# Latent attention's probabilities turned by transposing transfers out of SBUF

## The chip, the cores and the metric

The kernel runs on one core of a Trainium2 chip. A core has five engines, each with its own in-order instruction queue: TensorE (PE; its weight loads are counted apart as PEld), VectorE (DVE), ScalarE (ACT), GpSimd (POOL) and SyncE (SP), which issues transfers. The metric is the device time of one execution in microseconds.

## The reference

A decoder trunk of two layers over 256 rows of width 2048, in f32. Layer 0 has differential attention, layer 1 latent attention; each is followed by cross-attention into 256 memory rows and by a squared-ReLU MLP. The change touches the attention part of layer 1:

```python
def mla_attention(h, wdown, q_norm, kv_norm, wuq, wukv, wo, cos, sin):
    ...
    q = jnp.concatenate([q[..., :MLA_NOPE], apply_rope(q[..., MLA_NOPE:], cos, sin)], axis=-1)
    ...
    def block(qi, q0):
        s = jnp.einsum('bqhd,bkhd->bhqk', qi, k).astype(jnp.float32) * scale
        s = jnp.where(causal_mask(q0, S), s, -jnp.inf)
        p = jax.nn.softmax(s, axis=-1).astype(v.dtype)
        return jnp.einsum('bhqk,bkhd->bqhd', p, v)
```

There are 16 heads of 128 columns plus 64 rotary ones, and query blocks of 128 rows.

## The kernel before

Every product is done in three passes: each f32 operand is split into a high half (a rounded copy, by ScalarE) and a low half (the rest, by VectorE), and high x high, high x low and low x high are added in PSUM. Weights arrive by SP's queue in tiles `raw` of 128 x 2048 (1 MB, seven buffers), and are split in pieces of 1024 columns into `whi` (L221, ScalarE) and `wlo` (L222, VectorE), four buffers of each. TensorE reads one such pair in a run of twelve matmuls of 512 columns; a fifth split waits until the first pair has been read.

Latent attention goes in four groups of four heads (0 to 3). For each group, `project_latent` makes queries, keys and values, `attend4` the attention, and `project_group` adds the group's part of the output projection one group later. Within `attend4` there are four blocks: two pairs of heads p, two query tiles t. Tile t = 0 has 128 keys (256 probabilities a row for a pair), t = 1 has 256 (512 a row). A block (`probs`) does these steps: TensorE's scores into a PSUM bank (`ax`); VectorE's mask, maximum and scale, ScalarE's two exponentials (L619), VectorE's reciprocal and product (L680), which leave the probabilities in a tile `p`; TensorE's flips of `p`, two or four transposes of 128 x 128 (L174, from L684) back into the same bank; ScalarE's high half (L687) and VectorE's low half (L688) into a tile that the products with the values (`weighted`) read.

The queries' rotary parts are turned in the same stretch (`rotary_queries`): GpSimd rotates them, ScalarE copies a rounded half into a tile `ev` (L1721), VectorE adds the rest (L1722), TensorE flips eight blocks of it. The rotary queries of groups 2 and 3 are made while group 1 is in its softmax. During group 3, ScalarE also scales rows of the memory (`memT`, L416) for the next cross-attention.

`p`, `ev`, the `planes` below and some others share one set of seven buffers (EVS).

What sets the order: TensorE's order is the order in which the code emits it. Side tasks (generators) are put between the matmuls of the main stream by a clock of estimated times; a `yield` names the time after which the task may go on (T_SM after a softmax, a slack for each group, T_TURN after a turn). The other engines' queues are ordered at build time by the framework's scheduler, from estimates of its own, and this order is fixed. SP's loads stay in program order. An instruction that waits holds up all that is behind it on its engine.

The kernel has a transposing path through DRAM in other places: ScalarE parts the 16-bit halves of f32 words into two planes (L377), GpSimd writes them to DRAM (L379), SP's transposing transfer brings them back turned (L384).

Of the kernel before, what the change touches and what calls it, by code (L numbers as in the profile page):

```python
# [10 lines left out]
F32 = mybir.dt.float32  # L11
F32R = mybir.dt.float32r
I32 = mybir.dt.int32
U16 = mybir.dt.uint16
# [4 lines left out]
P = 128  # L19
# [3 lines left out]
CH = 512  # L23
# [7 lines left out]
EVS = 7  # L31
# [3 lines left out]
T_EV, T_TURN, T_ROT, T_SM, T_SQ, T_ADD, T_NORM, T_SUM, T_BATCH, T_STORE, T_LAND, T_DMA, T_SHORT = 2.6, 2.6, 12.0, 6.5, 4.4, 2.2, 7.2, 3.0, 17.0, 22.0, 7.0, 8.0, 11.0  # L35

URGENT = 250
NEG = -1.0e30
LAMBDA_INIT = 0.8 - 0.6 * math.exp(-0.3 * 0)
SC_DA = 1.0 / math.sqrt(128)  # L40
# [12 lines left out]
def trunk(ctx, tc, x, xT, xT0, mem, memT, positions, gcols, gfinal, lam_vecs, consts, W, out):  # L53
    nc = tc.nc

    def pool(name, bufs, space=None):
        kw = {"space": space} if space else {}
        return ctx.enter_context(tc.tile_pool(name=name, bufs=bufs, **kw))
# [5 lines left out]
    work = pool("work", 2)  # L64
# [6 lines left out]
    def nm(s):  # L71
        serial[0] += 1
        return f"{s}_{serial[0]}"
# [82 lines left out]
    def side_bank():  # L156
        while not free_banks[0]:
            yield 0.5
        free_banks[0] -= 1
        return bank()  # L160

    def give_back():
        free_banks[0] += 1

    def mmul(o, stationary, moving, start, stop, onto=False):
        n = 1
        for d in moving.shape[1:]:
            n *= d
        clock[0] += max(0.11, n / 2400 + 0.0133)
        return nc.tensor.matmul(o, stationary, moving, start=start, stop=stop, skip_group_check=onto)  # L170

    def flip(o, src):
        clock[0] += 0.109
        nc.tensor.transpose(o, src, ident)  # L174

    def f32(ap):
        return ap.bitcast(F32)
# [6 lines left out]
    def urgent():  # L184

        return tc.high_priority(offset=URGENT)

# [6 lines left out]
    def raw_tile():  # L194
        return wraw.tile([P, 4 * CH], F32, tag="raw", name=nm("raw"))
# [186 lines left out]
    def turned_by_dma(there):  # L382
        landed = work.tile([P, 4, 2 * P], U16, tag="ev", name=nm("landed"), bufs=EVS)
        tc.keep_in_program_order(nc.sync.dma_start_transpose(landed, there))  # L384
        return landed.bitcast(F32).rearrange("p k t -> p k t")

    def split_landed(dst, t, src):
        at = slice(t * P, (t + 1) * P)
        hi = dst[:, 0, :, at]
        tc.keep_in_program_order(nc.scalar.copy(hi, src))  # L390
        nc.vector.tensor_tensor(dst[:, 1, :, at], src, f32(hi), ALU.subtract)  # L391
# [213 lines left out]
    def val(v, half, kb, lo, n):  # L605
        return v[:, half, 2 * kb : 2 * kb + 2, :].rearrange("p a b -> p (a b)")[:, lo : lo + n]
# [33 lines left out]
    def side_by_side(q, k, h):  # L640

        both = k[:, :, h, :P]
        return [(q[:, 0, h], (both,)), (q[:, 1, h], (both,))]

    def scores(view, blocks, t, causal):


        for b, pairs in enumerate(blocks):
            todo = [(q[:, t * P : (t + 1) * P], kk) for q, ks in pairs for kk in ks]
            for i, (q, kk) in enumerate(todo):  # L650
                mmul(view[:, b], q, kk, i == 0, i == len(todo) - 1)
        if causal:
            last = view[..., view.shape[-1] - P :]
            nc.vector.tensor_tensor(last, last, masks(len(blocks)), ALU.add)

    def masks(n):
        return mask.unsqueeze(1).broadcast_to([P, n, P])

    def attend4(score_pairs, inputs, v, dst, causal, scales=(1.0, 1.0), slack=0.0):


        pTs = [raw_tile().bitcast(F32R).rearrange("p (a b c d) -> p a b c d", a=2, b=2, c=2) for _ in range(2)]

        def probs(t, p, nk):


            sb = yield from side_bank()
            heads = (2 * p, 2 * p + 1)
            pr = work.tile([P, CH], F32, tag="ev", name=nm("p"), bufs=EVS)[:, : 2 * nk]
            rows = pr.rearrange("p (h k) -> p h k", k=nk)  # L670
            if nk == P:
                view = sb.rearrange("p (h a k) -> p h a k", h=2, a=2)
                scores(view, [score_pairs(h, True) for h in heads], t, False)
                nc.vector.tensor_tensor(rows, view[:, :, 1], masks(2), ALU.add)
                nc.vector.tensor_tensor(rows, rows, view[:, :, 0], ALU.add)
                pr, rs = softmax(pr, 2, pr, scales[t])
            else:
                scores(sb.rearrange("p (h k) -> p h k", k=nk), [score_pairs(h, False) for h in heads], t, causal)
                pr, rs = softmax(sb, 2, pr, scales[t])
            nc.vector.tensor_tensor(rows, rows, rs[:, :2].unsqueeze(2).broadcast_to([P, 2, nk]), ALU.mult)  # L680
            yield T_SM + slack
            nb = nk // P
            for i in range(2 * nb):
                flip(sb[:, i * P : (i + 1) * P], pr[:, i * P : (i + 1) * P])  # L684
            src = sb[:, : 2 * nk].rearrange("p (h b q) -> p h b q", h=2, b=nb)
            hi = pTs[p][:, 0, :, :nb, t * P : (t + 1) * P]
            nc.scalar.copy(hi, src)  # L687
            nc.vector.tensor_tensor(pTs[p][:, 1, :, :nb, t * P : (t + 1) * P], src, f32(hi), ALU.subtract)  # L688
            give_back()
            yield T_TURN  # L690

        def weighted(po, p, i, kb, passes, first, last):
            vt = v() if callable(v) else v
            q = slice(kb * P if causal else 0, S)
            o = po[:, i * S : (i + 1) * S][:, q]
            for j, (sv, sp) in enumerate(passes):
                mmul(
                    o, val(vt, sv, kb, (2 * p + i) * P, P), pTs[p][:, sp, i, kb, q],
                    first and j == 0, last and j == len(passes) - 1,
                )  # L700

        def result(p, po):
            hi = dst[:, 0, 2 * p : 2 * p + 2, :]
            src = po.rearrange("p (h q) -> p h q", h=2)
            with urgent():
                nc.scalar.copy(hi, src)
                nc.vector.tensor_tensor(dst[:, 1, 2 * p : 2 * p + 2, :], src, f32(hi), ALU.subtract)

        PASSES = ((0, 0), (0, 1), (1, 0))

        def task():
            for i in inputs:
                yield i
            blocks = []
            for p in range(2):
                for t in range(NT):
                    blocks.append(Task(probs(t, p, P if causal and t == 0 else S)))
                    yield 1.3
            for b in blocks:
                yield b  # L720
            if causal:
                for p in range(2):
                    po = yield from side_bank()
                    for i in range(2):
                        for kb in range(2):
                            weighted(po, p, i, kb, PASSES, kb == 0, kb == 1)
                    result(p, po)
                    give_back()
                    yield 1.3
            else:  # L730
                pos_ = []
                for p in range(2):
                    pos_.append((yield from side_bank()))
                while not v():
                    yield 0.5
                for p in range(2):
                    for i in range(2):
                        weighted(pos_[p], p, i, 0, PASSES, i == 0, False)
                for p in range(2):
                    for passes in (PASSES[:2], PASSES[2:]):  # L740
                        for i in range(2):
                            weighted(pos_[p], p, i, 1, passes, False, passes == PASSES[2:] and i == 1)
                    result(p, pos_[p])
                    give_back()
            yield T_TURN

        dst.run(task())
# [859 lines left out]
    krope = Held(raw_tile().bitcast(F32R)[:, : 2 * S].rearrange("p (k t) -> p k t", k=2))  # L1607
# [37 lines left out]
    rq = keep2(rs, SC_MLA, "rq")  # L1645
# [99 lines left out]
    slacks = [4.5, 2.5, 2.5, 2.5]  # L1745

    def attend_latent(held, o):
        qr, q, k, v = held
        attend4(
            lambda h, first: side_by_side(q, k, h) + [(qr[:, h], (krope[:, :, :P],))]  # L1750
            if first
            else whole(q, k, h, S) + [(qr[:, h], (krope[:, 0], krope[:, 1]))],
            qr.tasks + q.tasks + k.tasks + krope.tasks, v, o, True, rq, slacks.pop(0),
        )

    norm, m, mk = attention(project_latent, attend_latent, sooner, G_CROSS + 16)
# [81 lines left out]
def _layout(i):  # L1838
# [16 lines left out]
    c[:, C_ID : C_ID + P] = np.eye(P, dtype=np.float32)  # L1855
    c[:, C_MASK : C_MASK + P] = np.where(q[None, :] <= q[:, None], 0.0, NEG)
    inv = [500000.0 ** (-(np.arange(0, r, 2)) / r) for r in (DA_ROT, MLA_ROPE)]
# [49 lines left out]
```

## Time and profile before

| what | value |
|---|---|
| median of 3 runs | 2172.3 us (2171.3 to 2172.62) |
| profiled execution, first to last instruction | 2169.0 us, granted clock 0.999 |
| TensorE busy | 2155.4 us (99%) |
| weight loads | 1805.5 us (83%) |
| VectorE busy | 1740.2 us (80%) |
| ScalarE busy | 1465.6 us (68%) |
| GpSimd busy | 221.0 us (10%) |
| DMA queue of SP's transfers | 440.14 MB, 56.9% of the span |

The profiled execution is told by its span alone; the runs' times also hold what lies before the first and after the last instruction. Latent attention lies between about 1200 and 1375 us: the scores of groups 0 to 3 begin at 1220, 1251, 1301 and 1348 us. A row of the chain of waits gives a start, a length and what ended last there; a row of instruction groups gives engine, operation, tiles written and read, and durations in ns as least, median and greatest.

### The profile page before, as it was taken

The page shows a single profiled execution, that of the slowest core. Times are in us where ns is not written, and L with a number is a line of the kernel's source. Part 1 is how long each engine was busy: PE and PEld are TensorE (multiplying, and loading weights), DVE is VectorE, ACT ScalarE, POOL GpSimd, SP SyncE. Part 2 cuts the span into 40 slices and gives each one's busy share as a digit, 9 for nine tenths or more (in the row PEclk, how much of TensorE's full clock was granted, in tenths as well). Part 3 has the DMA queues.
Part 4 walks back from the last instruction along what each step waited for, and adds up shares of the span by engine and source line. Part 5 has one row for each costly group of instructions (what it writes and reads, how often), then busy time and mean ns, then how long its engine had stood idle before and what let it go on. Part 6 is the DMA issues. An engine that isn't in the chain of part 4 may idle for free.

```text
span 2169.0 us, 27519 instructions
## 1 busy us (share of the span) xinstructions
PE 2155.4 (99%) x10187; PEld 1805.5 (83%) x10187; DVE 1740.2 (80%) x1962; ACT 1465.6 (68%) x1938; POOL 221.0 (10%) x336
## 2 busy tenths in 40 slices
PE   9999999999999999999999999999999999999998
PEld 7888888888888888888889988888888888888887
DVE  6656878788788889788886878778888888888887
ACT  7556756666767777776665755666777778677665
POOL 1113210001000000000000420000000000000001
PEclk9999999999999999999999999999999999999999
DMA  9477896548989999998986344645998999999895
GB/s 386 151 248 234 260 293 222 194 151 267 297 280 267 308 282 256 319 274 260 306 251 218 103 170 155 221 168 182 283 299 292 258 317 280 266 285 310 254 315 149
DMA packets 151863, 543.89 MB, mean 251 GB/s; under 512 B 79536, under 2 KB 79920, under 8 KB 92848
## 3 DMA queue, kind: packets, MB, share of 16 engines
q1 hardware_dynamic: 134496, 440.14, 56.9%
q0 software_dynamic: 16800, 101.20, 22.5%
q8 instruction: 80, 1.31, 0.2%
q10 hardware_dynamic: 432, 0.79, 0.1%
q14 instruction: 55, 0.45, 0.1%
HBM read 505.38 MB, written 19.40 MB: 242 GB/s over the span
## 4 chain that ended last, share of the span: by engine, by line
PE 95%; DVE 3%; DMA 1%; issue 1%; ACT 0%; DVEq 0%; POOLq 0%; POOL 0%
PE mm L170 62%; PE pr L170 28%; PE ax L170 3%; DVE wlo L222 1%; DMA raw<-in_mlp_wup_dram 1%; PE ax L174 1%; PE mm L174 1%; DVE raw L887 0%; DVE unit L391 0%; ACT whi L221 0%; DVE x L545 0%; DMA raw<-in_da_wqkv_dram 0%; PE pr L174 0%; DVE p L680 0%; DVE ev L1722 0%
## 5 line engine op out<-in xcount | busy, mean ns | idle before, releaser
L222 DVE TENSOR_TENSOR wlo<-raw,whi 128x1024 fp32r<-128x1024 f32 (+3 forms) x946 | 1138.8, 1217 | 335.5 <-ACT whi L221 313.7
L221 ACT CAST whi<-raw 128x1024 fp32r<-128x1024 f32 (+2 forms) x945 | 985.3, 1045 | 576.8 <-PE mm L170 420.0
L170 PE MATMUL mm<-whi,unit 128*128 128x512 f32 (+2 forms) x4000 | 1271.2, 389 | 1.3 <-DVE unit L391 0.9
L170 PEld LDWEIGHTS mm<-whi,unit 128*128 128x128 f32 x4000 | 749.1, 188 | 149.6 <-DVE unit L391 1.7
L170 PE MATMUL mm<-wlo,unit 128*128 128x512 f32 (+2 forms) x2000 | 774.1, 387 | 0.2
L170 PE MATMUL pr<-whi,unit 128*128 128x512 f32 x1912 | 610.5, 389 | 0.0
L170 PEld LDWEIGHTS mm<-wlo,unit 128*128 128x128 f32 x2000 | 376.2, 188 | 72.8 <-DVE wlo L222 3.0
L170 PEld LDWEIGHTS pr<-whi,unit 128*128 128x128 f32 x1912 | 358.8, 188 | 73.4
L170 PE MATMUL pr<-wlo,unit 128*128 128x512 f32 x956 | 372.3, 389 | 1.5 <-DVE wlo L222 1.5
L170 PEld LDWEIGHTS pr<-wlo,unit 128*128 128x128 f32 x956 | 179.7, 188 | 40.0 <-DVE wlo L222 3.6
L379 POOL DMA_DIRECT2D turned<-planes x66 | 37.7, 572 | 673.5 <-ACT planes L377 661.2
L887 DVE TENSOR_TENSOR raw<-raw,raw 128x2048 f32<-128x2048 f32 x40 | 91.5, 2288 | 8.8 <-DMA raw<-in_mlp_wup_dram 8.6
L545 DVE TENSOR_TENSOR x<-x,mm 128x512 f32<-128x512 f32 x128 | 85.3, 682 | 14.1 <-PE mm L170 14.0
L879 POOL DMA_DIRECT2D raw<-in_mlp_wup_dram x48 | 43.4, 905 | 447.8 <-DVE wlo L222 445.2
L431 POOL TENSOR_TENSOR rs<-rs,mhalf 128x1 f32<-128x1 f32 (+1 forms) x26 | 24.9, 962 | 408.1 <-DVE rs L430 408.0
L222 DVE TENSOR_TENSOR wlo<-unit,whi 128x1024 fp32r<-128x1024 f32 x48 | 57.3, 1221 | 5.2 <-ACT whi L221 4.0
L221 ACT CAST whi<-unit 128x1024 fp32r<-128x1024 f32 x48 | 49.8, 1053 | 9.7 <-PE pr L170 9.7
L377 ACT COPY planes<-p 128x1024 uint16<-128x1024 uint16 x48 | 50.0, 1041 | 0.3
L170 PE MATMUL mm<-unit,whi 128*128 128x256 f32 x256 | 46.9, 285 | 0.0
L425 ACT ACTIVATE junk<-x 128x512 bf16<-128x512 f32 (+1 forms) x57 | 35.3, 620 | 10.1 <-DVE x L1092 5.0
L1457 ACT ACTIVATE p<-p,r 128x512 f32<-128x512 f32 x42 | 30.4, 724 | 16.4 <-DVE p L962 7.4
L170 PEld LDWEIGHTS mm<-unit,whi 128*128 128x128 f32 x256 | 40.2, 192 | 0.3
(199 smaller groups left out, 1280.7 us busy)
## 6 DMA issues: line engine op xcount, KB each, us to landing
raw<-in_mlp_wdown_dram SPq DMA_DIRECT2D x128, 1024.0 KB, 7.3
raw<-in_mlp_wup_dram SPq DMA_DIRECT2D x120, 1024.0 KB, 6.9
raw<-in_mlp_wup_dram POOLq DMA_DIRECT2D x48, 1024.0 KB, 9.1
raw<-in_da_wqkv_dram SPq DMA_DIRECT2D x45, 1024.0 KB, 9.8
turned<-planes POOLq DMA_DIRECT2D x66, 256.0 KB, 6.4
raw<-in_da_wo_dram SPq DMA_DIRECT2D x16, 1024.0 KB, 7.0
raw<-in_ca_wkv_dram SPq DMA_DIRECT2D x16, 1024.0 KB, 6.7
raw<-in_mlp_wdown_dram POOLq DMA_DIRECT2D x16, 1024.0 KB, 10.7
```

Source lines behind the costliest of these rows:

```text
L170: return nc.tensor.matmul(o, stationary, moving, start=start, stop=stop, skip_group_check=onto)
L174: nc.tensor.transpose(o, src, ident)
L221: nc.scalar.copy(hi, r)
L222: nc.vector.tensor_tensor(lo, r, f32(hi), ALU.subtract)
L377: nc.scalar.copy(planes, src.bitcast(U16).rearrange("p (w s) -> p s w", s=2))
L379: nc.gpsimd.dma_start(there.rearrange("(q s) w -> q s w", s=2), planes)
L425: return nc.scalar.activation(junk[:, : src.shape[1]], src, AF.Square, scale=scale, accum_out=acc)
L431: nc.gpsimd.tensor_tensor(r[:, :n], r[:, :n], mhalf.broadcast_to([P, n]), ALU.pow)
L545: nc.vector.tensor_tensor(xc, xc, ps, ALU.add)
L879: tc.keep_in_program_order(nc.gpsimd.dma_start(onto, src, accum_op=ALU.add))
L887: nc.vector.tensor_tensor(o, o, q, ALU.add)
L1457: nc.scalar.activation(r, src, AF.Relu, scale=rstd[t])
```

## The change

In groups 1, 2 and 3 (the last argument is true when fewer than three slacks are left) TensorE no longer flips the probabilities. Instead ScalarE parts `p` into planes of 16-bit halves, in SBUF (`parted`); the PSUM bank is handed back after T_SM; after the group's slack + 1.5 a transposing transfer on SP's queue turns the planes into the place of `p` itself (`turned_here`); after T_JOIN ScalarE joins the halves to f32 words in the planes' place (`joined`); then high and low halves are taken as before, from SBUF. In the changed file, lines behind the new constant stand 1 later, those behind the new functions 23, those behind the block's new branch 32 or 33.

```diff
+T_JOIN = 4.6
...
+    def parted(src):
+        n = src.shape[1]
+        planes = work.tile([P, 2 * n], U16, tag="ev", name=nm("planes"), padded_shape=[P, 2 * CH], bufs=EVS)
+        nc.scalar.copy(planes.rearrange("p (s w) -> p s w", s=2), src.bitcast(U16).rearrange("p (w s) -> p s w", s=2))
+        return planes
+
+    def turned_here(planes, onto=None):
+        n = planes.shape[1]
+        if onto is None:
+            onto = work.tile([P, n], U16, tag="ev", name=nm("landed"), padded_shape=[P, 2 * CH], bufs=EVS)
+        else:
+            onto = onto.bitcast(U16)
+        landed = onto.rearrange("p (n t) -> p n t", t=P)
+        tc.keep_in_program_order(nc.sync.dma_start_transpose(landed, planes))
+        return landed
+
+    def joined(landed, planes):
+        n = landed.shape[1] // 2
+        words = planes.rearrange("p (k t s) -> p s k t", s=2, t=P)
+        nc.scalar.copy(words, landed.rearrange("p (s k) t -> p s k t", s=2))
+        return planes.bitcast(F32).rearrange("p (k t) -> p k t", t=P)
...
-            yield T_SM + slack
             nb = nk // P
-            for i in range(2 * nb):
-                flip(sb[:, i * P : (i + 1) * P], pr[:, i * P : (i + 1) * P])
-            src = sb[:, : 2 * nk].rearrange("p (h b q) -> p h b q", h=2, b=nb)
+            if sent:
+                planes = parted(pr)
+                yield T_SM
+                give_back()
+                yield slack + 1.5
+                landed = turned_here(planes, pr)
+                yield T_JOIN
+                src = joined(landed, planes).rearrange("p (h b) q -> p h b q", h=2)
+            else:
+                yield T_SM + slack
+                for i in range(2 * nb):
+                    flip(sb[:, i * P : (i + 1) * P], pr[:, i * P : (i + 1) * P])
+                src = sb[:, : 2 * nk].rearrange("p (h b q) -> p h b q", h=2, b=nb)
...
-            give_back()
-            yield T_TURN
+            if not sent:
+                give_back()
+            yield T_TURN + (1.0 if sent else 0.0)
...
-            qr.tasks + q.tasks + k.tasks + krope.tasks, v, o, True, rq, slacks.pop(0),
+            qr.tasks + q.tasks + k.tasks + krope.tasks, v, o, True, rq, slacks.pop(0), len(slacks) < 3,
```

ScalarE's queue in group 1, before: exponentials of the four blocks (L619), weight splits (`whi`), one cast of turned probabilities (L687), then the casts of the rotary `ev`.

```order
L619 ACTIVATE p_11005,ssum_11015<-p_11005,nmax_11014,rq_10090 128x128 x2
L221 CAST whi_10844<-raw_10842 128x1024
L619 ACTIVATE p_11030,ssum_11043<-ax_11029,nmax_11042,rq_10092 128x256 x2
L221 CAST whi_10848<-raw_10842 128x1024
L687 CAST raw_10990<-ax_11004 128x2x128
L619 ACTIVATE p_11058,ssum_11068<-p_11058,nmax_11067,rq_10090 128x128 x2
L221 CAST whi_10903<-raw_10901 128x1024
L619 ACTIVATE p_11083,ssum_11096<-ax_11082,nmax_11095,rq_10092 128x256 x2
L1721 CAST ev_11140<-ev_10966 128x4x64
L1721 CAST ev_11143<-ev_10967 128x4x64
```

The same place now, first half (L391 is the copy into planes, L407 the join, L719 the cast that was L687):

```order
L642 ACTIVATE p_11005,ssum_11015<-p_11005,nmax_11014,rq_10090 128x128 x2
L222 CAST whi_10844<-raw_10842 128x1024
L391 COPY planes_11023<-p_11005 128x512
L642 ACTIVATE p_11032,ssum_11045<-ax_11031,nmax_11044,rq_10092 128x256 x2
L407 COPY planes_11023<-p_11005 128x2x256
L222 CAST whi_10848<-raw_10842 128x1024
L391 COPY planes_11053<-p_11032 128x1024
L222 CAST whi_10903<-raw_10901 128x1024
L719 CAST raw_10990<-planes_11023 128x2x128
L642 ACTIVATE p_11062,ssum_11072<-p_11062,nmax_11071,rq_10090 128x128 x2
L407 COPY planes_11053<-p_11032 128x2x512
```

and, directly behind it, the second half:

```order
L222 CAST whi_10907<-raw_10901 128x1024
L719 CAST raw_10990<-planes_11053 128x4x128
L391 COPY planes_11080<-p_11062 128x512
L642 ACTIVATE p_11089,ssum_11102<-ax_11088,nmax_11101,rq_10092 128x256 x2
L407 COPY planes_11080<-p_11062 128x2x256
L391 COPY planes_11110<-p_11089 128x1024
L1754 CAST ev_11144<-ev_10966 128x4x64
L1754 CAST ev_11147<-ev_10967 128x4x64
```

The casts of `ev` stood behind the fourth pair of exponentials; now they stand behind three joins and four plane copies as well. On TensorE, the flips of this `ev` stand behind the same 30 matmuls of 512 columns as before; the eight flips of `p` that were among those are gone.

ScalarE's queue in group 3, now (L439 is the scaling of memT, before L416):

```order
L222 CAST whi_12124<-raw_12122 128x1024
L391 COPY planes_12074<-p_12056 128x512
L642 ACTIVATE p_12083,ssum_12096<-ax_12082,nmax_12095,rq_10092 128x256 x2
L222 CAST whi_12128<-raw_12122 128x1024
L407 COPY planes_12074<-p_12056 128x2x256
L222 CAST whi_12175<-raw_12173 128x1024
L391 COPY planes_12104<-p_12083 128x1024
L222 CAST whi_12179<-raw_12173 128x1024
L719 CAST raw_11979<-planes_12074 128x2x128
L407 COPY planes_12104<-p_12083 128x2x512
L439 ACTIVATE unit_12213<-raw_12214,g 128x256 x4
L719 CAST raw_11979<-planes_12104 128x4x128
```

Before, two weight splits stood between the fourth pair of exponentials of this group and its last cast (L687). Now the fourth plane copy stands behind the split whi_12175, and the last cast behind the fourth join and four scalings of rows (raw_12214) whose load SP issues behind the group's last transfer. The split four before whi_12175, whose buffer it takes over, is whi_11984: on TensorE, that one's run of twelve is followed by six matmuls, the products of the first pair, six matmuls, and the products of the second pair, which read the last cast's tile.

More of the change, by code (lines that the diff above doesn't have):

```diff
@@ L657, in masks, with attend4 @@
         return mask.unsqueeze(1).broadcast_to([P, n, P])
-    def attend4(score_pairs, inputs, v, dst, causal, scales=(1.0, 1.0), slack=0.0):
+    def attend4(score_pairs, inputs, v, dst, causal, scales=(1.0, 1.0), slack=0.0, sent=False):
         pTs = [raw_tile().bitcast(F32R).rearrange("p (a b c d) -> p a b c d", a=2, b=2, c=2) for _ in range(2)]
```

## The prediction

> **What bounds the kernel now.** I read the page's busy times first, then the chain that ended last, then the stretch of the latent attention (1150 to 1480 us) by windows and by its chain.
>
> ```profile
> span 2169.0 us, 27519 instructions
> PE 2155.4 (99%) x10187; PEld 1805.5 (83%) x10187; DVE 1740.2 (80%) x1962; ACT 1465.6 (68%) x1938; POOL 221.0 (10%) x336
> PE 95%; DVE 3%; DMA 1%; issue 1%; ACT 0%; DVEq 0%; POOLq 0%; POOL 0%
> ```
>
> TensorE is never free for long: its idle time is 2169.0 - 2155.4 = 13.6 us, start included. So whatever is taken off its queue is gained, and whatever makes it wait is lost, because no later slack gives it back. The median run, 2172.3 us, lies 3.3 us above this span; I leave that part as it is and add the sum to the median.
>
> The chain of waits of the stretch 1240 to 1300 us (start, length, what) shows the one place in it where something other than TensorE ends last:
>
> ```profile
> 1264.75 1.22 DVE wlo L222
> 1265.96 0.60 DVE x L545
> 1266.56 0.07 DVE rsum L624
> 1266.64 0.33 DVE ev L1722
> 1266.97 0.04 issue
> 1267.02 1.09 PE ax L174 x8
> ```
>
> The eight flips of the rotary rows (ev) wait for VectorE's ev, which follows ScalarE's cast of the same tile (L1721). In the windows (length, then TensorE, weight load, VectorE, ScalarE, GpSimd) that wait is the 0.46 us missing from TensorE's 15:
>
> ```profile
> 1260.00:1275.00 15.00, 14.54 (x80) 12.24 (x79) 13.96 (x25) 10.65 (x23) 4.29 (x7) 1.00 0.41 140
> 1350.00:1375.00 25.00, 25.00 (x142) 21.55 (x141) 24.38 (x49) 16.18 (x36) 0.00 (x0) 1.00 0.47 153
> ```
>
> **The change, part by part.** *Removed:* 36 flips of probabilities (12 in each of three groups).
>
> ```profile
> 1312.19 0.22 PE ax L174 x2
> 1315.17 0.44 PE ax L174 x4
> ```
>
> One costs 0.11 us of TensorE's path, so 36 x 0.11 = 4.0 us go, all of it on the engine that bounds.
>
> *Added to ScalarE:* 12 copies into planes and 12 joins, half of each kind over 1024 16-bit columns, half over 512.
>
> ```profile
> L377 ACT COPY planes<-p x48: 1037/1041/1047, 552.3 to 1993.5; 128x1024 uint16<-128x1024 uint16 x48
> L390 ACT CAST unit<-landed x52: 610/617/626, 546.0 to 2039.3; 128x512 fp32r<-128x512 f32 x52
> ACT whi L221 <- PE mm L170: 74.2, 63, 2.7
> ```
>
> A whole one is 1.04 us; a half one I price by a 512-column cast, 0.62. That is 12 x 1.04 + 12 x 0.62 = 19.9 us. As work it is hidden: from 1170 to 1480 us ScalarE waits 74.2 us for buffers of split weights that TensorE still reads. The first cast and VectorE's low half now read SBUF in place of PSUM; the cast's row above (0.62 from SBUF) against 0.57 below says that this is nothing. The plane copies' 12 transfers carry 2.3 MB in a stretch whose DMA share is under a half (0.41 and 0.47 above): hidden, and what they cost is their latency.
>
> *The new waits.* A join waits for a transfer, and it stands on ScalarE's in-order queue ahead of other work. The durations:
>
> ```profile
> landed<-turned SPq DMA_TRANSPOSE x2, 3.7
> turned<-planes POOLq DMA_DIRECT2D x2, 256.0 KB, 2.3
> L384 SPq DMA_TRANSPOSE landed<-turned x66: 1227/1634/9474, 115.1 to 2014.3; - x66
> DMA to landing us min/median/max: 3.1/6.0/14.0
> ```
>
> No row has a transpose out of SBUF. The same bytes through the same crossbar take 3.7 us in the quiet latent stretch (two of 256 KB), 3.1 at least and 6.0 in the median of all 66; a plain write of 256 KB takes 2.3. I take 3.7 for the whole (256 KB) and 3.1 for the half (128 KB), nearest in kind, and keep 2.3 and 6.0 as ends.
>
> The Trainium skill, VectorE: DVE Perf Modes, "The three transpose paths" and the rules behind it, speaks against this change: TensorE where PSUM will do as destination, the DMA crossbar otherwise, at 1309 ns for 128x128 in 16 bits. The trace has nothing that quick; if each landing took that, the walk below would end 4.8 us sooner (ScalarE's own work then fills the middle one) and the total would be about 2178 us, an estimate from that page.
>
> *Group 1 (from 1255 us).* ScalarE's new order is shown above: plane 0, join 0, plane 1, join 1, plane 2, join 2, plane 3, and only then the casts of the rotary ev. Each plane waits for the join before it, so three transfers stand in series. The start, and the pieces:
>
> ```profile
> 1255.77 1.04 ACT L221 CAST whi<-raw 128x1024 fp32r<-128x1024 f32 x1
> 1256.09 0.72 DVE L680 TENSOR_TENSOR p<-p,rsum 128x256 f32<-128x256 f32 x1
> L619 ACT ACTIVATE p<-ax,nmax,rq x12: 548/553/563, 1256.7 to 1361.9; 128x256 f32<-128x256 f32 x12
> L687 ACT CAST raw<-ax x13: 362/570/596, 1241.3 to 1366.7; 128x512 fp32r<-128x512 f32 x7, 128x256 fp32r<-128x256 f32 x6
> L1721 ACT CAST ev<-ev x6: 397/409/415, 1233.3 to 1268.2; 128x256 fp32r<-128x256 f32 x6
> L1722 DVE TENSOR_TENSOR ev<-ev,ev x6: 404/416/419, 1233.9 to 1270.8; 128x256 f32<-128x256 f32 x6
> ```
>
> Plane 0 starts at 1256.09 + 0.72 = 1256.81 and ends 1257.43; its transfer lands 1260.53; join 0 ends 1261.15, a weight split (1.05) 1262.20, plane 1 1263.24; landing 1266.94 (a split, a cast and two exponentials, 1.05 + 0.36 + 1.1 = 2.5 us, lie under it); join 1 1267.98, split 1269.03, cast 1269.60, plane 2 1270.22; landing 1273.32; join 2 1273.94, plane 3 1274.98, ev cast 1275.39, VectorE's ev 1275.81. TensorE comes to these flips after the same 30 matmuls as before, but without 0.46 of waiting and without eight p flips: 1267.02 - 0.46 - 0.88 = 1265.7. So it stands 10.1 us, 9.7 more than before. With 2.3 us a landing it is 7.3 (net 6.8; ScalarE's 2.5 us then end the middle wait), with 6.0 it is 18.2 (net 17.7).
>
> *Group 3 (from 1350).* Here plane 3 stands behind the split whi_12175, which needs the buffer of the split four before it, whi_11984. TensorE reads that one until its next-to-last run of matmuls before the group's products; from there it has 1.43 + 1.33 + 1.43 = 4.2 us left:
>
> ```profile
> 1241.16 2.77 PE mm L170 x12
> ...
> 1368.71 1.33 PE ax L170 x12
> 1370.04 1.43 PE mm L170 x6
> ```
>
> The first row is a whole run of twelve, 2.77. The loads and scalings of memT (the issues, a quiet landing of one load, four scalings on ScalarE):
>
> ```profile
> 1338.04 0.80 SPq L189 DMA_DIRECT2D raw<-in_memT_dram  x2
> raw<-in_memT_dram SPq DMA_DIRECT2D x8, 256.0 KB, 3.2
> 1375.79 1.71 ACT L416 ACTIVATE unit<-raw,g 128x256 fp32r<-128x256 f32 x4 [2.37 <-DMA raw<-in_memT_dram]
> ```
>
> In that time ScalarE must do the split 1.05 and plane 3 1.04; then comes the transfer and its join (3.7 + 1.04), or, slightly later, the memT rows whose load SP issues behind the transfer (1.23 + 0.4 + 3.2 = 4.8); then four scalings of memT 1.71 and the last cast 0.57: 9.2 us, a stall of 5.0. With 2.3 and a prompt memT it is 3.5, with 6.0 it is 7.2.
>
> *Group 2 (from 1300).* No rotary flips stand in it, and plane 3 comes two runs of weights sooner: 2 x 2.77 + 4.2 = 9.7 us of TensorE's work against 1.05 + 1.04 + 3.7 + 1.04 + 1.05 + 0.57 = 8.5. Nothing at 3.7; 1.1 us at 6.0.
>
> *Restart.* The granted clock stays 1.00 in the windows, but the kernel's first matmuls, out of idleness, are slow:
>
> ```profile
> 1.23 4.02 PE L1244 MATMUL ax<-blank 128*128 128x512 bf16 x9 [1.23 <-DVE coef L1332]
> ```
>
> Nine of them take 4.02 us where the later pace (2.77 for twelve, above) gives 9 x 0.231 = 2.08: a restart costs 1.9 us. I count it once, for the stall of 10 us. The Trainium skill, TensorE: Matmul & The Clock Gate, "What's actually happening", says that after one idle window of about 3.4 us the array runs at half rate for about as long; by that rule the 5 us stall pays too. No run shown so far has a restart in the middle of the kernel.
>
> *Sum:* -4.0 + 9.7 + 5.0 + 0 + 1.9 = +12.6; 2172.3 + 12.6 = **2185 us** (2184.9).
>
> SP's queue is no term: the 12 issues (1.23 us each, the minimum above) and their waits push weight loads back, but those wait for buffers, not the buffers for them; ScalarE's only wait for a load in the stretch is memT's, 2.37 us above. Without that cover each late load would cost what it is late.
>
> **Rivals.** (a) *Both stalls restart slowly*, by the mechanism just priced: +1.9, 2186.8; against it, the second stall is half the first. (b) *Dear transfers:* landings near the median of 66, 6.0, because weight loads share the 16 engines: -4.0 + 17.7 + 7.2 + 1.1 + 3.8 = +25.8, 2198. Against it, that median comes from batches of three in crowded stretches. (c) *Quick transfers,* 2.3, no slow restart: -4.0 + 6.8 + 3.5 = +6.3, 2178.6. (d) *One short stall that eats the gain:* if the rotary flips are late by only some 4 us and group 3 is not, the time stays at 2172. (e) The other side: *the joins never hold anything up*. Then 4.0 + 0.46 us go, 2167.8. ScalarE's 74.2 us of waiting speak for it; against it, the place: the ev casts must be ready 8.9 us after plane 0 starts, while the copies, splits and casts ahead of them take 0.62 + 0.62 + 1.05 + 1.04 + 2.5 + 1.04 + 1.05 + 0.57 + 0.62 + 0.62 + 1.04 + 0.83 = 11.6 without any landing. It decides only if that work, not just the transfers, moves elsewhere. That the change isn't there is out: the flips are gone from the order.
>
> **How the numbers follow.** Forecast 0.45 (own range 2180 to 2190), (a) 0.15, (b) 0.12, (c) 0.13, (d) 0.10, (e) 0.05. Differences under 0.2%, 4.3 us, can't be told from none here: slower 0.84, same 0.12, faster 0.04; most of (e) lies just beyond the edge. Range 2175 to 2198: below it (d) and (e), above it a part of (b).
>
> **What would show it.** Right: TensorE idle some 10 us before the rotary flips near 1266 us and some 5 us before the second products of group 3 near 1375; ScalarE's joins waiting for DMA in both; the flips of p down from 112 to 76; landings of p of 3 to 4 us; TensorE's total busy time down by about 4 us. Wrong: TensorE's idle time near 14 us as before; landings under 2.5 or above 5 us; VectorE or a late weight split, rather than a join, named ahead of the stalls; a slow pace of matmuls behind no stall, or behind both.

## The result and the profile after

The changed kernel takes 2188.65 us (median of 4 runs, 2185.17 to 2190.26), the kernel before on the same chip 2172.46 (4 runs, 2171.3 to 2173.58): a ratio of 1.0078, 95% interval 1.0066 to 1.0089. That is slower, as forecast, 3.7 us above the 2185.0 and inside the range. The profiled execution has a span of 2183.4 us, 14.4 more than before; it is the shortest of the four (2183.4 to 2188.2). The page of the changed kernel, busy times and shares of the chain:

```profile
span 2183.4 us, 27496 instructions
PE 2156.4 (99%) x10151; PEld 1804.8 (83%) x10151; DVE 1742.2 (80%) x1962; ACT 1486.0 (68%) x1962; POOL 220.3 (10%) x336
PE 91%; DMA 3%; DVE 3%; issue 1%; ACT 1%; POOL 1%; DVEq 0%; POOLq 0%; ACTq 0%; SPq 0%
```

TensorE is idle for 2183.4 - 2156.4 = 27.0 us, where it was 13.6: 13.4 more. It has 36 matmuls fewer, 4.0 us of work, and yet is busy 1.0 us longer, so other matmuls have become 5.0 us slower. 13.4 - 4.0 + 5.0 = 14.4, the whole difference of the spans. ScalarE has 20.4 us more work.

Where TensorE stands: the waits of the stretch 1170 to 1480 us (engine, line, what it waited for; us in total, times, longest):

```profile
ACT whi L222 <- PE mm L171: 62.1, 53, 2.2
...
ACT planes L407 <- DMA p<-planes: 9.8, 10, 2.5
...
PE ax L175 <- DVE ev L1755: 8.9, 2, 8.7
...
PE ax L171 <- ACT raw L719: 4.7, 1, 4.7
...
PE ax L171 <- DVE raw L720: 0.9, 1, 0.9
```

The three PE rows are group 1's rotary flips, group 3's second products and group 2's second products. The granted clock (the last but two of a windows row) tells of the slower matmuls; both long waits have it (0.72 and 0.86), and before the change it was 1.00 in every window of the stretch:

```profile
1260.00:1275.00 15.00, 6.33 (x30) 5.23 (x29) 10.11 (x20) 11.64 (x23) 3.15 (x6) 0.72 0.47 120
...
1375.00:1400.00 25.00, 20.11 (x90) 16.69 (x89) 16.27 (x26) 17.23 (x28) 0.00 (x0) 0.86 0.60 215
```

TensorE's rows at the two places (in brackets the idle time before and what ended it):

```profile
1273.22 1.94 PE L175 MATMUL ax<-identr,ev 128*128 128x128 f32 x8 [8.67 <-DVE ev L1755]
...
1391.30 3.34 PE L171 MATMUL ax<-raw,unit 128*128 128x256 f32 x12 [4.75 <-ACT raw L719]
```

Eight flips take 1.94 us in place of 1.09. Counted over the 160 matmuls behind each gap, against the usual distance between starts of the same shape (0.227 us for 512 columns, 0.120 for 256, 0.109 for a flip), the slow pace costs 1.8 us behind the first gap and 2.6 behind the second (the 2.7 of the expectations below still held a gap of 0.14), 4.4 of the 5.0 above. By groups: group 1 is -1.3 for 12 flips + 8.2 (8.67 less the old 0.46) + 1.8 = +8.7; group 2 is -1.3 + 0.9 = -0.4; group 3 is -1.3 + 4.9 + 2.6 = +6.2; together 14.5.

ScalarE's queue in group 1, of the same profile, from the second block's join on (L407 joins, L391 plane copies, L1754 the rotary casts):

```profile
1264.85 1.33 ACT L407 COPY planes<-p 128x1024 uint16<-128x1024 uint16 x1 [0.50 <-DMA p<-planes]
...
1267.51 0.61 ACT L391 COPY planes<-p 128x512 uint16<-128x512 uint16 x1
...
1270.65 0.76 ACT L407 COPY planes<-p 128x512 uint16<-128x512 uint16 x1 [1.42 <-DMA p<-planes]
1271.28 1.03 ACT L391 COPY planes<-p 128x1024 uint16<-128x1024 uint16 x1
1272.22 0.71 ACT L1754 CAST ev<-ev 128x256 fp32r<-128x256 f32 x2
```

The order is the one that the prediction walked through, but ScalarE waits for landings only 1.41 (the first join, at 1258.98) + 0.50 + 1.42 = 3.3 us of the whole way.

In group 3 no landing ends a wait in the chain that ends at the second products. Pieces of it:

```profile
1385.13 1.44 PE mm L171 x6
...
1386.59 0.99 ACT whi L222
...
1387.85 1.33 ACT planes L407
1389.18 1.17 ACT unit L439 x3
```

The first row is TensorE's last run before it stands. The weight split that follows it, whi_12179, stands behind the fourth plane copy in ScalarE's queue; it waited 2.12 us for the buffer that this run still read. The last transfer landed at 1387.54, while the split ran; then came a cast, the last join, the four scalings and the last cast. So TensorE stood for work queued behind a split that waited for TensorE.

The prices of the pieces, by form, and the landings of the twelve transfers:

```profile
L407 ACT COPY planes<-p 128x1024 uint16<-128x1024 uint16 x6 | 8.1, 1348 | 4.6 <-DMA p<-planes 4.6
L391 ACT COPY planes<-p 128x1024 uint16<-128x1024 uint16 x6 | 6.2, 1039 | 0.0
L407 ACT COPY planes<-p 128x512 uint16<-128x512 uint16 x6 | 4.7, 776 | 5.2 <-DMA p<-planes 5.2
```

```profile
DMA to landing us min/median/max: 2.4/2.7/5.9
```

### The profile page after: what moved, and what is told of

The parts are those of the page before. It is cut to its first block, busy times and chain, and to the rows that moved or that the text cites. A ratio compares the mean times of both kernels' runs of the same rounds, so it can differ in the third digit from the quotient of the medians.

```text
span 2183.4 us, 27496 instructions
## 1 busy us (share of the span) xinstructions
PE 2156.4 (99%) x10151; PEld 1804.8 (83%) x10151; DVE 1742.2 (80%) x1962; ACT 1486.0 (68%) x1962; POOL 220.3 (10%) x336
## 4 chain that ended last, share of the span: by engine, by line
PE 91%; DMA 3%; DVE 3%; issue 1%; ACT 1%; POOL 1%; DVEq 0%; POOLq 0%; ACTq 0%; SPq 0%
PE mm L171 59%; PE pr L171 27%; DMA raw<-in_mlp_wup_dram 2%; PE ax L171 2%; DVE wlo L223 2%; PE ax L175 1%; PE mm L175 1%; DMA p<-planes 1%; DVE raw L920 1%; ACT whi L222 1%; DVE unit L414 0%; DVE x L568 0%; PE ax L1277 0%; ACT planes L391 0%; ACT planes L407 0%
```

## The experiments

Ratios (with their 95% intervals) are against runs of the kernel before on the same chip; "+" is slower, in us between medians. The two are estimated apart and differ by up to 1.2 us, so that a difference near nothing can have another sign than its ratio.

### One group at a time

```diff
-            ... slacks.pop(0), len(slacks) < 3,
+            ... slacks.pop(0), len(slacks) == 2,      # 1, 0 in the other two
```

> Only group 1's probabilities (from about 1255 us) go by transfer; groups 2 and 3 are flipped as before. Theory (the stalls are local: group 1 is held up by its joins ahead of the rotary casts): -1.3 (12 flips) + 8.2 (8.67 us of idleness before the rotary flips, 0.46 before) + 2.1 (half of the 4.2 us that the two slow restarts seem to cost) = +9.0 against the kernel before. Rival (the loss is spread: 20 us more work on ScalarE, 12 more transfers on the queues, each group paying alike): a third of +16.2, +5.4.

> Only group 2's probabilities (from about 1300 us) go by transfer. Theory: -1.3 (12 flips) + 0.9 (the gap before its second products) and no slow restart = -0.4, that is no change that can be measured. Rival (spread loss): +5.4.

> Only group 3's probabilities (from about 1350 us) go by transfer. Theory: -1.3 (12 flips) + 4.8 (the gap before its second products) + 2.1 (a slow restart) = +5.6. Rival (spread loss): +5.4, so this run alone does not tell the two apart; with the runs of groups 1 and 2 it does. If the second stall restarts at full speed it is +3.5.

Measured: group 1 alone +9.3 (1.0046, 1.0031 to 1.0061), group 2 alone +0.4 (1.0000, 0.9991 to 1.0010), group 3 alone +9.5 (1.0046, 1.0029 to 1.0063). The loss is local: a spread one would have shown in group 2. Group 1 came as expected, with the same gap of 8.67. Group 3 did not: 9.5 in place of 5.6. Its waits and, from ScalarE's rows, the join of its second block, the memory rows' scaling and the last cast:

```profile
PE ax L171 <- ACT raw L719: 7.4, 1, 7.4
```

```profile
1368.30 1.35 ACT L407 COPY planes<-p 128x1024 uint16<-128x1024 uint16 x1 [3.45 <-DMA p<-planes]
...
1383.04 1.71 ACT L439 ACTIVATE unit<-raw,g 128x256 fp32r<-128x256 f32 x4 [0.87 <-DMA raw<-in_memT_dram]
1384.65 0.60 ACT L719 CAST raw<-planes 128x512 fp32r<-128x512 f32 x1
```

SP's queue at that time (a 1 MB weight load, the second to fourth transfer, the memory rows), and the landings of the four transfers:

```profile
1357.63 0.42 SPq L190 DMA_DIRECT2D raw<-in_ca_wkv_dram  x1
1360.11 18.84 SPq L401 DMA_TRANSPOSE p<-planes  x3
1378.99 1.06 SPq L190 DMA_DIRECT2D raw<-in_memT_dram  x2
```

```profile
DMA to landing us min/median/max: 2.4/2.7/8.1
```

The second block's transfer was issued 2.5 us behind the weight load, and its join began 8.2 us after that. The memory rows' loads stood behind the last transfer, and ScalarE waited for them ahead of the last cast. The gap of 7.4 is followed by 3.7 us of slow pace. In this run, then, group 3 was held up longer by a landing behind a load and by the memory rows; the 4.75 of the full change is another case, with neither at its end.

### The flips alone

```diff
-                planes = parted(pr)
                 ...
-                landed = turned_here(planes, pr)
                 yield T_JOIN
-                src = joined(landed, planes)...
+                src = pr...
```

> The 36 flips are left out and nothing is put in their place: the first cast and the low half read the probabilities unturned (that part of the computation, the turning, is left out). It measures the term -4.0 of the sum. If each flip costs its 0.11 us of the engine that bounds: -4.0, or -4.5 with the old wait of 0.46 us, 2168.0 against 2172.5. Rival (the flips lie in waits of TensorE, or ScalarE and VectorE are late without them anyway): within 1 us of no change.

Measured -1.1 (0.9994, 0.9985 to 1.0003): the rival, no change. TensorE's waits of the stretch, then two of ScalarE's rows:

```profile
PE ax L175 <- DVE ev L1753: 2.8, 2, 2.6
```

```profile
1264.04 0.57 ACT L642 ACTIVATE p<-ax,nmax,rq 128x256 f32<-128x256 f32 x1 [0.33 <-DVE nmax L640]
...
1265.14 1.01 ACT L1752 CAST ev<-ev 128x256 fp32r<-128x256 f32 x3
```

The rotary flips wait 2.6 us where they waited 0.46. Their casts stand behind the exponentials of group 1's last block, and these wait for VectorE's maximum; that chain does not become shorter when TensorE has less to do, so TensorE only comes to it earlier. The 2.6 us are also followed by a slow pace (1.5 us by the same count). So in the profiled execution some 3.6 of the 4.0 us are gone again (2.6 - 0.46 + 1.5) before anything is added.

### Landings or copies

Three kernels take the change apart: copies without transfers, transfers without copies, transfers with plane copies but no joins. In all three TensorE's order is that of the change; ScalarE's and VectorE's are what the framework's scheduler then makes of them, so their details differ, and what a landing would cost in one fixed order is not shown.

```diff
-                landed = turned_here(planes, pr)
                 yield T_JOIN
-                src = joined(landed, planes)...
+                src = joined(planes, pr.bitcast(U16))...
```

> All three groups with their plane copies and joins, but without the 12 transfers: a join reads the planes and writes the place of p (the turning is left out of the computation; the order of TensorE is that of the change). It separates the landings from ScalarE's added work. In the changed kernel's group 1 ScalarE stands 1.41 + 0.50 + 1.42 = 3.3 us for landings ahead of the rotary casts. Theory 1 (both count): group 1's gap falls from 8.67 by 3.3 to about 5.4, its slow restart (1.8) stays, group 3's gap of 4.75 loses the 3.4 us between plane 3 and its join: about 1, with little restart; group 2's 0.87 goes. Total -4.0 + 5.4 - 0.46 + 1.8 + 1 = about +4 against before, 2176. Theory 2 (the landings are all of it): gaps as before, -4.0 and a little, 2169. Theory 3 (ScalarE's added work is all of it, the landings are hidden): as the changed kernel, +16.

Measured +16.5 (1.0079, 1.0064 to 1.0094): theory 3, as much as the changed kernel. TensorE's waits, and the chain that ends at the rotary flips:

```profile
PE ax L175 <- DVE ev L1754: 8.5, 2, 8.2
PE ax L171 <- ACT raw L718: 6.2, 1, 6.2
```

```profile
1269.97 1.12 DVE wlo L223
1271.09 0.34 DVE p L703
...
1271.51 0.62 ACT planes L391
1272.13 1.11 ACT p L642 x4
1273.24 0.66 ACT p L407
```

No landing is left, and the gap is 8.2 all the same. ScalarE now waits 2.26 us for the third block's p, which VectorE made late behind a weight split's low half; then this block's plane copy, the last block's exponentials, a join, a cast and the last block's plane copy follow each other to the rotary casts. Group 3's 6.2 has no landing in it either. Where a landing ended the wait in the changed kernel, VectorE ends it here a little later.

```diff
-                planes = parted(pr)
                 ...
-                landed = turned_here(planes, pr)
+                landed = turned_here(pr.bitcast(U16))
                 yield T_JOIN
-                src = joined(landed, planes)...
+                src = landed...                      # as many 16-bit numbers
```

> The other half of the run without transfers: all 12 transfers, but none of ScalarE's 24 copies. p itself is the source of the transfer, what lands goes into a buffer of its own, and the cast and the low half read as many 16-bit numbers of it as they read floats before (parting and joining are left out of the computation). A block still takes two buffers. Theory (ScalarE's and VectorE's work, in their orders, sets the stalls; the run without transfers was +16.5): group 1's gap as in the run without flips, 2.6, and one more weight split ahead of the rotary casts, 1.05, with a restart of 1.5 to 2; group 3's at most 1: -4.0 + 3.7 - 0.46 + 1.8 + 1 = about +2 against before. Rival (the landings, or the two buffers of a block, are enough for the stalls): +8 or more.

Measured -0.8 (1.0002, 0.9993 to 1.0011): no change; the theory's +2 lies within the interval (-1.5 to +2.4 us), the rival's +8 far outside. The rotary flips wait 1.7 and 1.35 us; group 3 has no wait. TensorE's waits, then the first two casts of probabilities on ScalarE:

```profile
PE ax L175 <- DVE ev L1754: 3.3, 3, 1.7
```

```profile
1273.70 0.41 ACT L718 CAST raw<-landed 128x256 fp32r<-128x256 uint16 x1 [1.84 <-DMA landed<-p]
1276.81 0.62 ACT L718 CAST raw<-landed 128x512 fp32r<-128x512 uint16 x1 [2.70 <-DMA landed<-p]
```

ScalarE still waits for landings, 1.84 and 2.70 us, but behind the rotary casts, where nothing that TensorE needs soon is queued: these waits cost nothing.

```diff
                 landed = turned_here(planes, pr)
                 yield T_JOIN
-                src = joined(landed, planes)...
+                src = landed...                      # as many 16-bit numbers
```

> The changed kernel with its plane copies and transfers but without the 12 joins: the cast and the low half read as many 16-bit numbers of p's place, where the transfer lands, as they read floats before (joining is left out of the computation). It splits the copies, whose absence alone brought the time back to that of before. Theory 1 (planes and joins count alike, as work in series with the exponentials and with VectorE's p on the way to the rotary casts): walked by the changed kernel's rows, plane 2 ends at 1267.0, the exponentials of block 3 at 1268.1, its p at 1269.3, plane 3 at 1270.3, the rotary cast at 1270.7, the flips at 1271.5 against 1273.2: a gap near 7, with a restart of 1.8; group 3 loses a join and a landing ahead of its last cast, its gap about 2 with a restart of 1.5: -4.0 + 6.5 + 1.8 + 2 + 1.5 = about +8. Rival (it is the joins, standing for landings on ScalarE's queue): +1 to +3.

Measured +9.6 (1.0042, 1.0028 to 1.0056): theory 1, with gaps of 7.28 (near 7 expected) in group 1 and 1.96 + 0.99 (2) in group 3. TensorE's wait at the rotary flips, and two of ScalarE's rows:

```profile
PE ax L175 <- DVE ev L1755: 7.5, 2, 7.3
```

```profile
1267.39 0.62 ACT L391 COPY planes<-p 128x512 uint16<-128x512 uint16 x1 [1.24 <-DVE p L703]
...
1270.12 1.04 ACT L391 COPY planes<-p 128x1024 uint16<-128x1024 uint16 x1 [1.01 <-DVE p L703]
```

Each of these plane copies waits for VectorE's p; the last block's exponentials wait behind the first of them, the rotary casts behind the second. Without the joins group 1's gap is only 1.4 us shorter, group 3's 1.8.

Together: with the copies the stall is there with or without transfers, without any of the copies group 1's gap is about 3 us with or without them (1.7 + 1.35 here, 2.6 in the run without flips), group 3 has none, and the flips' 4.0 us pay for it. In group 1 it is ScalarE's copies, standing between the exponentials of one block and of the next, and ahead of the rotary casts, in series with VectorE's p. Whether another order of the same copies on ScalarE, with the rotary casts ahead of them, would do without the stall was not run and stays open.

### Seven buffers

```diff
+        half = n < CH
-        planes = work.tile(..., tag="ev", ..., bufs=EVS)
+        planes = work.tile(..., tag="junk" if half else "ev", ..., bufs=1 if half else EVS)
```

> The planes of 512 columns get a buffer of their own (a spare tile of 1 KB that holds thrown-away squares elsewhere) in place of one of the seven ev buffers. Nothing else is changed; with it ScalarE's order becomes plane 0, plane 1, join 0 (plane 1 no longer behind join 0), and the exponentials of block 3 stand ahead of join 1. Theory (the seven buffers, two of them held by the rotary rows, put the copies and joins in series: a block takes two of them where it took one): landings overlap, group 1's rotary flips come 2.5 to 3 us sooner (gap about 6), group 3's products 1 to 3 us sooner: total 3 to 6 us below the changed kernel, about +12 against before. Rival (the buffers don't matter, ScalarE's work and each block's own landing do): within 1.5 us of the changed kernel, +16.

Measured +8.9 (1.0043, 1.0026 to 1.0060), a little more than the theory allowed (3 to 6 us below the changed kernel was expected, 7 it is), with the expected +12 inside the interval. TensorE's waits:

```profile
PE ax L175 <- DVE ev L1756: 6.1, 2, 5.9
PE ax L171 <- ACT raw L720: 2.2, 1, 2.2
PE ax L171 <- DVE raw L721: 1.0, 1, 1.0
```

With two tiles less in each group taken from the shared set, the scheduler could put the last block's exponentials ahead of the second block's join. So the order that made the series was not the code's but the buffers': a block holds p and planes, two of the seven, where it held one.

### The slow pace behind a stall

```diff
                 b = yield from side_bank()
+                for _ in range(70 if filled and t == 0 else 0):
+                    nc.tensor.transpose(b[:, :P], ident, ident)
                 ...
                     po = yield from side_bank()
+                    for _ in range(35 if p and last else 0):
+                        nc.tensor.transpose(po[:, :P], ident, ident)
```

> The changed kernel with 70 idle turnings of the identity (0.109 us each, 7.6 us) on TensorE right ahead of group 1's rotary flips and 35 (3.8 us) ahead of group 3's second products, into the banks that these fill next; ScalarE's and VectorE's orders are unchanged. TensorE is then busy where it stood, so only the price of the slow restarts can change. In the changed kernel's trace the 160 matmuls behind the two gaps take 1.8 and 2.7 us longer than at their usual pace. Theory (idleness itself sets off the slow pace): both go, total 4.5 us below the changed kernel, about +11.7 against before, and a granted clock of 1.00 in 1260 to 1300 and 1375 to 1400. Rival (the slow pace has another cause, or waits of 1 us already set it off): as the changed kernel, +16 within 1.

Measured +15.9 (1.0071, 1.0056 to 1.0086): no gain over the changed kernel that the times could show. The trace of this kernel, TensorE's waits, one window, and the fillers with the flips behind them:

```profile
PE ax L171 <- ACT raw L719: 1.8, 2, 1.0
PE ax L175 <- DVE ev L1758: 1.7, 2, 1.5
PE ax L171 <- DVE raw L720: 1.3, 2, 1.0
```

```profile
1375.00:1400.00 25.00, 23.69 (x134) 20.33 (x133) 16.33 (x26) 16.31 (x29) 0.00 (x0) 1.00 0.55 150
```

```profile
1268.01 7.80 PE L1764 MATMUL ax<-identr 128*128 128x128 f32 x70
1277.34 1.09 PE L175 MATMUL ax<-identr,ev 128*128 128x128 f32 x8 [1.53 <-DVE ev L1758]
```

Idleness does set off the slow pace: with TensorE kept busy the clock is 1.00 and the eight flips take 1.09. But not all of the 4.4 us is kept. Group 2's second products, which TensorE now reaches sooner, wait 0.84 + 0.96 in place of 0.87, and group 3's, behind their fillers, another 0.97 + 0.34: the joins end when ScalarE ends them. From the stretch's start to its end this execution needs about 2 us less than the changed kernel's. The rest of its span is no measure (2.33 us were lost at 550 us, where 0.45 is usual). What the pace costs in the end, between about 2 us and 4.4, stays open.

### The places moved

```diff
-            yield T_EV
+            yield T_EV + (9.0 if gi == 2 and i == 0 else 0.0)       # rotary flips
             ...
-            yield T_TURN + (1.0 if sent else 0.0)
+            yield T_TURN + (last if sent else 0.0)                  # last: 7.0 in group 3
```

> The changed kernel with two places moved on TensorE: group 1's rotary flips stand 42 matmuls (42 x 0.227 = 9.5 us) later, group 3's products about 6 us later; other matmuls that are ready fill the time. On ScalarE three more weight splits (3 x 1.05 us) then stand ahead of the rotary casts. Theory (the stalls are a matter of place: TensorE has other work while the joins land): group 1's gap 8.67 - 9.5 + 3.1 = about 2.3, with a restart of 1.5, group 3's about 0, group 2's 0.9: total -4.0 + 2.3 - 0.46 + 1.5 + 0.9 = about 0 against before (2171 to 2176). Rival (ScalarE is short in this stretch, so whatever TensorE takes in between waits for its splits too): over +10.

> The kernel before (all flips on TensorE) with the same two places moved: group 1's rotary flips 9 us and group 3's products 6 us later on the planner's clock. It is the control for the run in which both were moved in the changed kernel (-1.7, interval -2.8 to +1.3). Theory (the move only takes away waits; the kernel before has one of 0.46 us there): -0.5, no change that can be measured. Rival (the move itself is worth more than that, and the transfers nothing): -2 or more.

> The changed kernel with both cures: the two places moved on TensorE and the planes of 512 columns in a buffer of their own. With the places moved alone, gaps of 0.24 (group 1) and 0.15 + 0.96 (group 2) were left. Theory (with more room the joins stand further ahead of what needs them, so those go): -4.0 for the flips and at most 0.5 for the old wait: -3.5 to -4.5 against before. Rival (the order on ScalarE that the buffer brings puts other work late, as its wait for weight buffers did): 0 or more.

Measured: the change with both places moved -1.7 (0.9996, 0.9987 to 1.0006); the kernel before with the same move -0.1 (1.0001, 0.9992 to 1.0010), so the move alone is worth nothing that these runs could show; the change with the move and the half planes' own buffer -4.0 (0.9980, 0.9971 to 0.9989, 11 runs against 27). Moving the places thus all but ends the stalls, as the theory had it, and the rival's +10 is out. The last kernel is faster than the one before and than the changed one. Its waits and a window:

```profile
PE ax L175 <- DVE ev L1756: 0.2, 1, 0.2
```

```profile
1260.00:1275.00 15.00, 15.00 (x72) 12.58 (x71) 14.16 (x26) 13.10 (x25) 6.47 (x11) 1.00 0.41 111
```

From 1260 to 1400 us TensorE does not stand at all (the 0.2 lies at 1237.6, as in the kernel before). The 36 flips then bring the 4.0 us that they cost, as far as the interval tells (-6.3 to -2.4 us); what the buffer adds to the move is within the noise of the two.

## Why the prediction was right, and where it was wrong

- *"-4.0 (36 flips)"*: right as TensorE's work, since the last experiment gets it. Taken away alone they bring 1.1, because the rotary flips wait for a chain that is not TensorE's.
- *"Group 1, +9.7"*: the size was near (8.67 - 0.46 = 8.2; flips at 1273.2 in place of the 1275.8 walked), the reason was not. "Three transfers stand in series" was true of the order, but the landings ended only 3.3 us of ScalarE's waiting, and without them the gap is 8.2 still. The step that failed is "as work it is hidden": ScalarE's 62 to 74 us of waiting for weight buffers are spread over the stretch, while the way from one block's exponentials over VectorE's p to the next block's had no room for a plane copy and a join. The list of 11.6 us under rival (e) had the copies in it but not VectorE's p between them, so it priced the stall without landings at 2.7, where the run showed 8.2, in an order of its own with 2.26 us of waiting for VectorE's p.
- *Prices*: landings were quicker than taken (2.4 for a half one, taken at 3.1; 3.0 to 3.6 and once 5.9 for a whole one, taken at 3.7), joins dearer (1.35 and 0.78 for 1.04 and 0.62). The errors offset each other. By the 1309 ns of the Trainium skill, VectorE: DVE Perf Modes, "The three transpose paths", the estimate was 2178; no landing was that short, and the run with no landing at all stood at +16.5, so a shorter one alone would not have brought it.
- *"Group 3, +5.0"*: 4.75 measured, and the last join, the scalings and the last cast stood at the end of the way as walked. But the middle term was another: the sum has the transfer and the memory rows' load there, and the run showed the split whi_12179, which could not start before TensorE had read its buffer (1386.59) and which the sum leaves out, with the landing 0.3 us ahead of the join behind it. The two are about as long, so the hit is partly luck; alone, group 3 stood 7.4.
- *"Group 2, 0"*: right within 0.9.
- *"Restart, 1.9, counted once"*: too small. Both stalls restarted slowly, 1.8 and 2.6: rival (a)'s mechanism, at more than its price. This and the spread between executions, not the stalls, are why the forecast lay low: 8.2 + 4.9 + 0.9 us of idleness are 0.7 less than the 14.7 forecast, the slow pace is 2.5 more, and the medians differ by 1.8 more than the profiled spans (16.2 and 14.4): 3.6 of the 3.7 us. Where the other executions of the changed kernel lose that 1.8 no trace shows. The Trainium skill, TensorE: Matmul & The Clock Gate, "What's actually happening", asks for an idle window of about 3.4 us. Both stalls are longer, and agree; but gaps of 2.6 us, and of 1.7 and 1.35 us close together, were also followed by a slow pace (1.5 and 1.9 us by the count above), so the measurement goes below that bound, while single gaps of up to 1.5 us were not (0.2).
- *Rival (e)*, that the joins hold nothing up, "decides only if that work, not just the transfers, moves elsewhere": this sentence was borne out by the run without copies.
- *"What would show it"*: both stalls came where they were expected, but TensorE's busy time rose by 1.0 us where it was to fall by about 4. Three signs of being wrong came too: landings of 2.4 us, below 2.5, and one of 5.9; in group 3 a late weight split ahead of the stall; and the slow pace behind both stalls.

## What to carry to other kernels

An engine that is idle a third of the time can still have no room between two steps of one chain: before moving work onto it, follow the chain through every engine that it touches, and price the work there, not as a share of the stretch. To learn whether a transfer's latency or the copies around it cost the time, take out each alone; here ScalarE's joins waited for the DMA, and the copies were the cause. A stall that is a matter of place can be moved away: emit the consumer later, where ready work stands, and give the new tiles a buffer that doesn't put the old ones in series.

## What the runs showed of the hardware

- A transposing transfer from SBUF to SBUF landed 2.4 us after its issue with 128 KB and mostly 3.0 to 3.1 with 256 KB. Two of 256 KB took 5.9 and 8.1 us, issued 2.5 us behind a 1 MB load on the same queue; they landed 1.0 and 2.3 us after that load. Another, in group 2, was issued 3.0 us behind a 1 MB load that landed sooner (5.1 us after its issue, against 7.4 and 8.2), and took 3.3.
- On ScalarE the same number of 16-bit words costs 1.04 us when the copy parts them (reads with a stride) and 1.35 when it joins them (writes with a stride); 0.61 and 0.78 for half.
- Waits of 2.6 us, and pairs of 1.4 to 1.7, are enough for TensorE to go on more slowly (granted clock 0.89 in 1260 to 1275 us, in the runs without flips and without copies); the 1.5 and 1.9 us lost there are more than half of the wait itself.
